# A streaming encoder step on one core: gain, mean and bias of the last normalization applied by TensorE, and other tiles in other buffers

## The chip, the cores and the metric

The kernel runs on one core of a Trainium2 chip. A run is one launch, and the time is the device time of that core in microseconds (us). Of the kernel before there are three runs, with a median of 2784.76 us, and one more execution that was profiled.

The engines are named as in the profile: PE is TensorE (PEld its weight loads), DVE is VectorE, ACT is ScalarE, POOL is GpSimd, SP the engine that issues most loads and stores. DMA stands for the transfers themselves. PSUM is the memory that products are written to, in eight banks of 512 columns; everything else on the chip lies in SBUF.

## The reference

One step of a two-layer encoder over 288 frames: 256 of a new stream and 32 of a running one. Each frame has 2048 features. The first layer mixes by a gated MLP, the second by retention; behind each comes a dense SwiGLU network (FFN), and behind each of these four parts a normalization:

```python
def layer_norm(x, g, b):
    mu = jnp.mean(x, axis=-1, keepdims=True)
    var = jnp.mean(jnp.square(x - mu), axis=-1, keepdims=True)
    return (x - mu) * lax.rsqrt(var + LN_EPS) * g + b

def swiglu(x, w_in, w_out):
    gate, up = jnp.split(x @ w_in, 2, axis=-1)
    return (jax.nn.silu(gate) * up) @ w_out

for i in range(2):
    h = gmlp_mix(x) if i == 0 else retention_mix(x)
    x = layer_norm(ALPHA * x + h, ln_mix_g[i], ln_mix_b[i])
    x = layer_norm(ALPHA * x + swiglu(x, w_ffn_in[i], w_ffn_out[i]), ln_ffn_g[i], ln_ffn_b[i])
```

The hidden width of the FFN is 5632. All is in 32-bit floats. The change concerns the last `layer_norm` alone, whose result is the output `y`.

## The kernel before

**Layout.** Activations are held with the features on the 128 partitions: 16 tiles (KT) of 128 features, each 128 x 288 with the frames as columns. A normalization over the features is therefore a sum over partitions and tiles; partitions are summed by a product with a constant matrix `one2048` that holds 1/2048, which leaves the mean of each frame in every partition.

**Weights.** All weight matrices are cut into blocks of 128x128 and packed in the order of use, eight blocks to a chunk of 512 KB. `prep` (L71) loads a chunk from DRAM into a tile `raw` on SP's queue, ScalarE casts it to a rounded high part `whi` (L559, in the helper `split`), VectorE subtracts to get the low part `wlo` (L560). The pool has three `raw` buffers, four `whi` and four `wlo`. `blk` (L90) asks for chunk c+3 when the first block of chunk c is taken.

**Products.** `step` (L110 to L112) makes three products of 288 columns per block: high by high, low activation by high weight, high activation by low weight. PE runs its instructions in the order in which they are written. The other engines' order is set by a planner that walks the program with estimated durations and lets an instruction go when what it needs is there, earlier written ones first. In a `manual_schedule` block the named engines too keep the written order.

**The two FFNs.** `ffn` (L704) makes half of the hidden tiles (22 of 44), multiplies them by their part of the output weights, then does the other half. In the second FFN a tile `hid` holds the high and low parts of the hidden tiles side by side. The last four output tiles (12 to 15, ENDS) of the second half are not made there but in `ending`.

**The ending.** `ending` (L424) first calls `ahead` (L331), then goes over tiles 12 to 15 and 22 hidden tiles each: a product of 288 columns with the low weight (L436) and a `paired` one (L437) that takes high and low hidden parts for the first half of the frames (144 columns of each). The weight chunks are kept: for the first seven, `whi` lies in room of the activation tiles `xl` and `xh`, which nobody needs any more. A second pass (`second`, L445) makes the `paired` products for the other half of the frames, 4 tiles x 22. So the first half of the frames (h = 0) is complete one pass earlier and is normalized while PE does the second pass.

From there on VectorE, ScalarE and POOL run in written order (FINISH). For each tile `add` brings the PSUM sums into `yh`, `square` squares on ScalarE, `gather` (L355) adds tile and square into two running sums on VectorE. `means` (L372) multiplies the sums by `one2048`; `spread` (L387 to L396) makes the row of means and the row `a` = 1/sqrt(variance + eps). `rows` (L401) subtracts the mean or multiplies by `a`, up to four tiles at a time, `affine` (L408 on ScalarE, L410 on VectorE) applies gain and bias per feature, `store` (L413) writes out.

For the second half (h = 1), behind the last tile, PE does the subtraction for nine tiles: `lift` (L420, L421) multiplies each by the identity and adds the negative mean by a matrix whose first row is -1. VectorE then multiplies from PSUM (L490) three tiles at a time. Identity and the -1 matrix lie in a tile `centring`, which `ahead` takes from the pool tag `raw`.

Of the kernel before, what the change touches and what calls it, by code (L numbers as in the profile page):

```python
# [210 lines left out]
class PostNorm:  # L211
# [118 lines left out]

    def ahead(self, ms):  # L331
        nc = self.nc
        for m in ms:
            nc.vector.tensor_tensor(self.tile(m), self.tile(m), self.like(self.c), ALU.subtract)
# [13 lines left out]
    def square(self, h, m):  # L348
        self.sq = self.tmp(f"sq{h}_{m}")[:, :NH]
        self.nc.scalar.activation(self.sq, self.yh[:, h, m, :], AF.Square)  # L350

    def gather(self, h, m):
        s = self.s[:, :, h * NH:(h + 1) * NH]
        for i, d in enumerate((self.yh[:, h, m, :], self.sq)):
            self.nc.vector.tensor_tensor(s[:, i, :], s[:, i, :], d, ALU.add)  # L355

    def end(self, h, m, ps):
        self.add(h, m, ps)
        self.square(h, m)
        self.gather(h, m)  # L360

    def first(self, m, ps, both):
        y = self.tile(m)
        self.nc.vector.tensor_tensor(y, self.like(both[:, :NT]), y, ALU.add)
        self.end(0, m, ps)

    def means(self, h, parts):
        core, one = self.core, self.cst["one2048"]
        self.m = [core.bank(f"m{h}{i}")[:, :NH] for i in range(2)]
        for j, p in enumerate(parts):  # L370
            for m, r in zip(self.m, p):
                self.nc.tensor.matmul(m, one, r, start=j == 0, stop=j == len(parts) - 1)  # L372
# [5 lines left out]
    def spread(self, h, mids, between):  # L378

        nc, core = self.nc, self.core  # L380
        cols = slice(h * NH, (h + 1) * NH)
        m1, m2 = self.m
        self.scale, self.mean = self.a[:, cols], self.b[:, cols]
        self.ap = ap = core.bank(f"ap{h}")[:, :NH]
        v = core.bank(f"fin{h}")[:, :NH]
        t, r = self.tmp(f"t{h}")[:, :NH], self.tmp(f"r{h}")[:, :NH]
        nc.scalar.activation(t, m1, AF.Square)  # L387
        nc.scalar.copy(self.mean, m1)
# [9 lines left out]
    def rows(self, h, k, n, eng, op):  # L398
        f = {ALU.subtract: (self.m[0], self.mean), ALU.mult: (self.ap, self.scale)}[op][eng is self.nc.gpsimd]
# [14 lines left out]

    def lift(self, h, k, n):

        mm = self.nc.tensor.matmul
        off = self.core.accum(f"off{k}")[:, :n * NH].rearrange("p (k n) -> p k n", n=NH)
        for i in range(n):
            mm(off[:, i, :], self.ident, self.yh[:, h, k + i, :], start=True, stop=False)  # L420
            mm(off[:, i, :], self.minus, self.mean, start=False, stop=True)  # L421
        return off

    def ending(self, w, koff, x):  # L424
# [24 lines left out]
        def quad(k, eng=dve):  # L449
            self.rows(0, k, 4, eng, ALU.subtract)  # L450
            self.rows(0, k, 4, eng, ALU.mult)

        def out(k):
            self.affine(0, k, 4)
            self.store(0, k, 4)

        with core.tc.manual_schedule(engines=FINISH):
# [17 lines left out]
            self.add(1, KT - 1, ps[KT - 1])  # L475
            self.square(1, KT - 1)
            self.means(1, [self.sum_rows(1), (self.yh[:, 1, KT - 1, :], self.sq)])
            off = {}

            def mids():  # L480
                for k in (2, 5, 8):
                    off[k] = self.lift(1, k, 3)
                self.rows(1, 12, 4, gps, ALU.subtract)

            self.spread(1, mids, lambda: self.rows(1, 0, 2, dve, ALU.subtract))
            self.rows(1, 12, 4, gps, ALU.mult)

            def lifted(k):
                y = self.yh[:, 1, k:k + 3, :]
                dve.tensor_tensor(y, off[k], self.scale.unsqueeze(1).broadcast_to([P, 3, NH]), ALU.mult)  # L490

            lifted(2)
            self.rows(1, 0, 2, dve, ALU.mult)
            self.affine(1, 2, 3)
            self.store(1, 2, 3)
            lifted(5)
            self.affine(1, 0, 2)
            self.store(1, 0, 2)
# [686 lines left out]
```

## Time and profile before

| | |
|---|---|
| median of the three runs | 2784.76 us (2783.88 to 2784.85) |
| the profiled execution, its own time | 2786.61 us |
| its span, first to last instruction | 2784.8 us |
| mean granted clock of TensorE | 0.998 |
| PE busy | 2771.0 us, 21,614 instructions |
| VectorE, ScalarE, POOL busy | 1702.9, 1252.3, 138.9 us |
| read and written in DRAM | 487 and 25 MB, 184 GB/s over the span |
| ending: first product, last large product | 2727.6 and 2765.6 us from the span's start |
| last store issued | 2781.2 us |

A row of the chain of waits is: start, duration, engine, what it writes, the line, and how many were merged. A row of the timeline is: start, duration, engine, line, operation, out<-in, shapes, count, and in brackets how long the engine had been idle before and what ended that. A row for a stretch has the stretch, its length, then the busy time of PE, PEld, DVE, ACT and POOL with their counts, the granted clock of TensorE (1.00 is full), the busy share of the DMA engines and GB/s. Products in 32-bit floats show as two records each; the large ones as one.

### The profile page before, as it was taken

What the parts mean: (1) busy time and instruction counts of PE and PEld (TensorE: products, weight loads), DVE (VectorE), ACT (ScalarE), POOL (GpSimd) and SP (SyncE); (2) the same over time, 40 slices, a digit from 0 to 9 for tenths busy, and PEclk for the clock granted to TensorE, in tenths of its full rate; (3) what the DMA queues carried; (4) which work ended last, traced back from release to release, by engine and by line L of the source; (5) the groups of instructions that cost most, each with busy time, mean ns of one, the idle gap of its engine ahead of it and who ended that gap; (6) DMA issues with size and microseconds to landing.
All of it is one profiled execution on the core that took longest, in us unless ns stands there. A gap on an engine that the chain in (4) does not pass through costs nothing.

```text
span 2784.8 us, 51601 instructions
## 1 busy us (share of the span) xinstructions
PE 2771.0 (100%) x21614; PEld 2760.1 (99%) x21614; DVE 1702.9 (61%) x2497; ACT 1252.3 (45%) x1680; POOL 138.9 (5%) x239
## 2 busy tenths in 40 slices
PE   9999999999999999999999999999999999999998
PEld 9999999999999999999999999999999999999997
DVE  6688964445444466968765676767954444444465
ACT  5455554333333344645443444445644333343344
POOL 1100000000000000012200111200000000000000
PEclk9999999999999999999999999999999999999999
DMA  8654555555555555567765676765555555555553
GB/s 279 219 186 163 171 174 175 174 174 174 172 174 172 179 177 175 176 216 233 225 208 172 197 224 205 233 199 173 168 174 174 174 168 173 174 172 173 173 174 110
DMA packets 146585, 515.51 MB, mean 185 GB/s; under 512 B 18016, under 2 KB 20464, under 8 KB 146320
## 3 DMA queue, kind: packets, MB, share of 16 engines
q1 hardware_dynamic: 131984, 473.33, 51.3%
q0 software_dynamic: 14224, 38.59, 4.7%
q8 instruction: 169, 2.77, 0.4%
q14 instruction: 64, 0.52, 0.1%
q10 hardware_dynamic: 144, 0.29, 0.0%
HBM read 486.98 MB, written 25.17 MB: 184 GB/s over the span
## 4 chain that ended last, share of the span: by engine, by line
PE 98%; DVE 1%; DMA 1%; ACT 0%; issue 0%; DVEq 0%; POOL 0%; ACTq 0%; POOLq 0%
PE af_in L110 13%; PE af_in L112 13%; PE af_in L111 13%; PE ab_in L110 7%; PE ab_in L112 7%; PE ab_in L111 7%; PE af_out L111 6%; PE af_out L112 6%; PE af_out L110 6%; PE aa_in L112 2%; PE aa_in L110 2%; PE aa_in L111 2%; PE ab_out L110 2%; PE ab_out L111 2%; PE ab_out L112 2%; PE aa_out L111 1%
## 5 line engine op out<-in xcount | busy, mean ns | idle before, releaser
L560 DVE TENSOR_TENSOR wlo<-raw,whi 128x1024 fp32r<-128x1024 f32 (+1 forms) x885 | 1076.1, 1218 | 851.1 <-ACT whi L559 846.4
L559 ACT CAST whi<-raw 128x1024 fp32r<-128x1024 f32 (+1 forms) x885 | 925.7, 1048 | 1320.8 <-PE af_in L111 324.2
L110 PE MATMUL af_in<-xh,whi 128*128 128x288 f32 (+1 forms) x2816 | 814.1, 289 | 0.0
L112 PE MATMUL af_in<-xh,wlo 128*128 128x288 f32 (+1 forms) x2816 | 813.8, 289 | 0.0
L111 PE MATMUL af_in<-xl,whi 128*128 128x288 f32 x2816 | 812.8, 289 | 0.0
L111 PEld LDWEIGHTS af_in<-xl,whi 128*128 128x128 f32 x2816 | 528.6, 188 | 0.0
L112 PEld LDWEIGHTS af_in<-xh,wlo 128*128 128x128 f32 x2816 | 528.6, 188 | 0.0
L110 PEld LDWEIGHTS af_in<-xh,whi 128*128 128x128 f32 x2816 | 528.4, 188 | 0.0
L110 PE MATMUL ab_in<-xh,whi 128*128 128x288 f32 (+1 forms) x1536 | 445.4, 290 | 0.0
L112 PE MATMUL ab_in<-xh,wlo 128*128 128x288 f32 (+1 forms) x1536 | 444.0, 289 | 0.0
L111 PE MATMUL ab_in<-xl,whi 128*128 128x288 f32 x1536 | 444.0, 289 | 0.0
L111 PEld LDWEIGHTS ab_in<-xl,whi 128*128 128x128 f32 x1536 | 288.4, 188 | 0.9
L110 PEld LDWEIGHTS ab_in<-xh,whi 128*128 128x128 f32 x1536 | 288.2, 188 | 0.8
L112 PEld LDWEIGHTS ab_in<-xh,wlo 128*128 128x128 f32 x1536 | 288.4, 188 | 0.0
L112 PE MATMUL af_out<-hh,wlo 128*128 128x288 f32 x704 | 203.2, 289 | 0.0
L110 PE MATMUL af_out<-hh,whi 128*128 128x288 f32 x704 | 203.2, 289 | 0.0
L111 PE MATMUL af_out<-hl,whi 128*128 128x288 f32 x704 | 203.2, 289 | 0.0
L111 PE MATMUL af_out<-hid,whi 128*128 128x288 f32 x616 | 179.6, 292 | 0.0
L112 PE MATMUL af_out<-hid,wlo 128*128 128x288 f32 x616 | 179.3, 291 | 0.0
L110 PE MATMUL af_out<-hid,whi 128*128 128x288 f32 x616 | 177.2, 288 | 0.0
L110 PE MATMUL aa_in<-xh,whi 128*128 128x288 f32 x512 | 148.4, 290 | 0.0
L112 PE MATMUL ab_out<-r_oh,wlo 128*128 128x288 f32 x512 | 147.8, 289 | 0.0
(281 smaller groups left out, 3806.1 us busy)
## 6 DMA issues: line engine op xcount, KB each, us to landing
raw<-in_wpack_dram SPq DMA_DIRECT2D x887, 512.0 KB, 3.3
v_room<-tv POOLq DMA_DIRECT2D x32, 144.0 KB, 4.9
of<-o_room POOLq DMA_DIRECT2D x32, 144.0 KB, 5.2
vw<-v_room POOLq DMA_DIRECT2D x8, 512.0 KB, 5.9
out_st_s_dram<-sso POOLq DMA_DIRECT2D x16, 256.0 KB, 2.7
o_room<-to POOLq DMA_DIRECT2D x8, 512.0 KB, 3.3
out_st_p_dram<-so POOLq DMA_DIRECT2D x16, 256.0 KB, 5.3
y<-in_xT_dram SPq DMA_DIRECT2D x8, 288.0 KB, 4.9
```

Source lines behind the costliest of these rows:

```text
L110: mm(wide, hi, halves(xh, lead), start=first, stop=False)
L111: mm(halves(ps[:, lead:], 0, lead), hi, halves(xl), start=False, stop=False)
L112: mm(wide, lo, halves(xh, lead), start=False, stop=last)
L559: nc.scalar.copy(hi, f)
L560: nc.vector.tensor_tensor(lo, f, hi.bitcast(F32), ALU.subtract)
```

## The change

- **Tables.** A new method `tables`, called when the second FFN opens its pool, makes there the identity, 15 diagonal 128x128 blocks of the gain (`diag`, 15 ScalarE scalings of the identity), a tile `gb` with the gain in row 0 and the bias in row 32 (zeroed on POOL, then two loads of 8 KB on POOL's queue from a new input), and a zeroed tile `ms` of 64 x 144. `hid` lies behind these in the same pool, and the filler tile ahead of it shrinks from 44 to 36 floats.
- **No `centring`.** `ahead` no longer takes a `raw` buffer; the -1 matrix is gone.
- **First half.** The means are asked for after product 15 of the second pass's first tile rather than 19. POOL subtracts and multiplies for tiles 8 to 15 (before: 12 to 15), VectorE for 0 to 7 (before: 0 to 11). `affine` of tiles 8 to 11 goes to VectorE.
- **Sums of the second half.** `gather` is gone there. Tiles 12 to 15 and their squares are summed by PE, each as a further product with `one2048`, together with the running sums of tiles 0 to 11.
- **The close.** For tiles 1 to 15 PE multiplies by the diagonal gain block (`gained`) and then adds gain x (-mean) + bias x standard deviation by one product with `gb` and `ms`. VectorE multiplies the result by `a` from PSUM, three tiles at a time, and it is stored. Tile 0 goes by VectorE and ScalarE. All stores are on SP.

```diff
+    def tables(self, pool, rows):
+        nc = self.nc
+        ident = pool.tile([P, P], F32, name="ident")
+        make_identity(nc, ident)
+        self.diag = pool.tile([P, KT, P], F32, name="diag")
+        for k in range(1, KT):
+            nc.scalar.mul(self.diag[:, k, :], ident, self.gain(k))
+        self.gb = pool.tile([2 * NS, KT, P], F32, name="gb")
+        self.ms = pool.tile([2 * NS, NH], F32, name="ms")
+        nc.gpsimd.memset(self.gb, 0.0)
+        nc.gpsimd.memset(self.ms, 0.0)
+        for i in range(2):
+            nc.gpsimd.dma_start(self.gb[i * NS:i * NS + 1], rows[i:i + 1])
+
     def ahead(self, ms):
...
-        room = self.core.wp.tile([P, CB * P], F32, tag="raw", name="centring", bufs=3)
-        self.ident, self.minus = room[:, :P], room[:, P:2 * P]
-        make_identity(nc, self.ident)
-        nc.gpsimd.memset(self.minus, 0.0)
-        nc.gpsimd.memset(self.minus[:1, :], -1.0)
...
+    def mean(self, i, r, start=False, stop=False):
+        self.nc.tensor.matmul(self.m[i], self.cst["one2048"], r, start=start, stop=stop)
...
         with core.tc.manual_schedule(engines=FINISH):
             self.first(KT - 1, *ps[KT - 1])
-            second(KT - 4, {19: lambda: self.means(0, [self.sum_rows(0)])})
-            self.spread(0, lambda: None, lambda: self.rows(0, 0, 4, dve, ALU.subtract))
-            quad(12, gps)
-            self.end(1, KT - 4, ps[KT - 4])
+            second(12, {15: early})
+            self.spread(mids, lambda: self.rows(0, 0, 4, dve, ALU.subtract))
+            for k in (8, 12):
+                self.rows(0, k, 4, gps, ALU.mult)
+            self.add(1, 12, ps[12])
+            sums = [self.sum_rows(1), self.square(1, 12)]
             self.rows(0, 0, 4, dve, ALU.mult)
             out(0)
-            second(KT - 3)
-            quad(4)
+            second(13)
+            for op in (ALU.subtract, ALU.mult):
+                self.rows(0, 4, 4, dve, op)
             out(4)
-            self.end(1, KT - 3, ps[KT - 3])
-            second(KT - 2)
-            quad(8)
-            out(8)
+            self.add(1, 13, ps[13])
+            sums.append(self.square(1, 13))
+            second(14)
+            self.add(1, 14, ps[14])
+            sums.append(self.square(1, 14))
+            out(8, dve)
             out(12)
-            self.end(1, KT - 2, ps[KT - 2])
-            second(KT - 1)
...
+            second(15)
+            self.close(ps[15], sums)
+
+    def close(self, b, sums):
+        core, nc, m = self.core, self.nc, KT - 1
+        mm, dve = nc.tensor.matmul, nc.vector
+        self.add(1, m, b)
+        y, sq = self.square(1, m)
+        self.means(1)
+        for j, pair in enumerate(sums):
+            for i, r in enumerate(pair):
+                self.mean(i, r, j == 0)
+        self.mean(0, y, stop=True)
+        off = {}
+
+        def gained(k):
+            bank = core.bank if k == 10 else core.accum
+            off[k] = bank(f"off{k}")[:, :3 * NH].rearrange("p (k n) -> p k n", n=NH)
+            for i in range(3):
+                mm(off[k][:, i, :], self.diag[:, k + i, :], self.yh[:, 1, k + i, :], start=i == 0, stop=False, skip_group_check=True)
...
+        self.mean(1, sq, stop=True)
+        for k in (4, 1, 7, 10, 13):
+            gained(k)
+        m1, m2 = self.m
+        std = slice(NS, NS + 1)
+        nc.scalar.activation(t, m1, AF.Square)
+        nc.scalar.mul(self.ms[:1], m1[:1], -1.0)
+        dve.tensor_tensor(self.yh[:, 1, 0, :], self.yh[:, 1, 0, :], m1, ALU.subtract)
+        dve.scalar_tensor_tensor(v, m2, LN_EPS, t, ALU.add, ALU.subtract)
+        nc.scalar.activation(r, v, AF.Abs_reciprocal_sqrt)
+        dve.tensor_tensor(p, v, r, ALU.mult)
+        dve.scalar_tensor_tensor(q, p, -0.5, r, ALU.mult, ALU.mult)
+        dve.scalar_tensor_tensor(self.ms[std], q[std], 1.5, p[std], ALU.add, ALU.mult)
+        dve.scalar_tensor_tensor(a, q, 1.5, r, ALU.add, ALU.mult)
+        for k in (4, 1, 7, 10, 13):
+            for i in range(3):
+                mm(off[k][:, i, :], self.gb[:, k + i, :], self.ms, start=False, stop=i == 2, skip_group_check=True)
+            y = self.yh[:, 1, k:k + 3, :]
+            dve.tensor_tensor(y, off[k], a.unsqueeze(1).broadcast_to([P, 3, NH]), ALU.mult)
+            if k == 4:
+                d = self.yh[:, 1, 0, :]
+                dve.tensor_tensor(d, d, a, ALU.mult)
+                self.affine(1, 0, 1)
+            first = 0 if k == 1 else k
+            self.store(1, first, k + 3 - first)
...
-            pool.tile([P, 44], F32, name="shift_hid")
+            ln.tables(pool, rows)
+            pool.tile([P, 36], F32, name="shift_hid")
             hid = pool.tile([P, HH, 2 * ROW], F32R, name="hid")[:, :, LEAD:]
```

More of the change, by code (lines that the diff above doesn't have):

```diff
@@ L348, in square @@
     def square(self, h, m):
[L349 to L360, printed above, removed]
+        sq = self.tmp(f"sq{h}_{m}")[:, :NH]
+        self.nc.scalar.activation(sq, self.yh[:, h, m, :], AF.Square)
+        return self.yh[:, h, m, :], sq
     def first(self, m, ps, both):
@@ L364, in first @@
         self.nc.vector.tensor_tensor(y, self.like(both[:, :NT]), y, ALU.add)
[L365 to L372, printed above, removed]
+        self.add(0, m, ps)
+        for s, d in zip(self.sum_rows(0), self.square(0, m)):
+            self.nc.vector.tensor_tensor(s, s, d, ALU.add)
     def sum_rows(self, h):
@@ L398, in rows @@
     def rows(self, h, k, n, eng, op):
-        f = {ALU.subtract: (self.m[0], self.mean), ALU.mult: (self.ap, self.scale)}[op][eng is self.nc.gpsimd]
+        f = {ALU.subtract: (self.m[0], self.mean_row), ALU.mult: (self.ap, self.scale)}[op][eng is self.nc.gpsimd]
         y = self.yh[:, h, k:k + n, :]
@@ L447, in second, with early, out, mids @@
                     at[k]()
[L449 to L454, printed above, removed]
+        def early():
+            self.means(0)
+            for i, s in enumerate(self.sum_rows(0)):
+                self.mean(i, s, True, True)
+        def out(k, eng=None):
+            self.affine(0, k, 4, eng)
             self.store(0, k, 4)
+        def mids():
+            for k in (8, 12):
+                self.rows(0, k, 4, gps, ALU.subtract)
@@ L474, in ending @@
-            second(KT - 1)
[L475 to L498, printed above, removed]
-            lifted(8)
-            self.rows(1, 11, 1, dve, ALU.subtract)
-            self.rows(1, 11, 1, dve, ALU.mult)
@@ L701, in gmlp, with ffn @@
     return ln
-def ffn(core, cst, x, y, lnp, layer, prev, out=None):
+def ffn(core, cst, x, y, lnp, layer, prev, out=None, rows=None):
     tc, nc = core.tc, core.nc
```

41 lines of the change are left out of this document (16 added, 25 removed).

## The prediction

> **What bounds the kernel now.** I read the page first, then the chain of waits, the load queue, the stretches of the granted clock, and last the timeline of the end.
>
> ```profile
> span 2784.8 us, 51601 instructions
> PE 98%; DVE 1%; DMA 1%; ACT 0%; issue 0%; DVEq 0%; POOL 0%; ACTq 0%; POOLq 0%
> ```
>
> The span is one stream of TensorE products. What can be won without touching their number lies where the chain leaves PE, and that is in the last 45 us:
>
> ```profile
> 2743.24 4.63 DMA raw<-in_wpack_dram
> 2747.97 1.05 ACT whi L559
> 2749.05 1.24 DVE wlo L560
> 2750.33 0.40 PE q L436
> ...
> 2767.33 3.29 ACT y L408 x8
> 2770.62 0.22 ACT sq L350
> 2770.87 0.32 DVE sums L355
> 2771.23 1.89 PE m L372 x6
> ...
> 2778.63 0.61 DVE y L490
> ```
>
> Two places. First, the last weight chunk comes late: its load (4.63 us), cast and split, and PE waits. Second, after its last large product PE waits for eight ScalarE `affine`s (3.29 us), behind which the square and sum of tile 14 are queued.
>
> Why the load is late is in the timeline of the weight loads, VectorE's splits and the casts, with a load 50 us earlier, the queue's own waits (us in total, times, longest) and the page's row for the load (us to landing):
>
> ```profile
> 2690.65 0.33 SPq L78 DMA_DIRECT2D raw<-in_wpack_dram  x1
> 2697.30 1.05 ACT L559 CAST whi<-raw 128x1024 fp32r<-128x1024 f32 x1 [1.52 <-PE af_out L111]
> 2741.99 1.23 DVE L560 TENSOR_TENSOR wlo<-raw,whi 128x1024 fp32r<-128x1024 f32 x1 [0.95 <-ACT whi L559]
> 2743.24 0.33 SPq L78 DMA_DIRECT2D raw<-in_wpack_dram  x1
> SPq L78 <- DVE wlo L560: 27.8, 10, 3.8
> raw<-in_wpack_dram SPq DMA_DIRECT2D x887, 512.0 KB, 3.3
> ```
>
> The last load is issued at 2743.24, just when the split of the chunk two before it ends (2741.99 + 1.23). At 2690.65 a load was issued 6.65 us ahead of its cast, and that cast waited for PE, not for data. The pool of `raw` tiles has three buffers (L81); `ahead` (L334) takes one of them for `centring` and keeps it to the end, because `lift` reads it. From there two loads are in flight. Here SP is bound by buffers.
>
> The stretches (PE busy, PEld, DVE, ACT, POOL; then the clock):
>
> ```profile
> 2747.80:2751.10 3.30, 1.49 (x12) 1.27 (x11) 1.66 (x3) 1.27 (x2) 0.00 (x0) 1.00 0.00 0
> 2751.20:2754.50 3.30, 3.30 (x16) 3.30 (x15) 0.77 (x2) 0.00 (x0) 0.00 (x0) 0.50 0.00 0
> 2768.30:2771.60 3.30, 1.18 (x3) 0.83 (x4) 0.70 (x3) 2.54 (x7) 0.00 (x0) 0.50 0.26 96
> ```
>
> Each wait is paid twice: a stretch in which PE was busy 1.49 of 3.30 us is followed by one at clock 0.50, and the wait before the means puts them at half clock too.
>
> **The change part by part.**
>
> *The third `raw` buffer.* `ahead` no longer takes `centring`; its identity goes into the FFN's own pool. Loads may again be issued three chunks ahead. The waiting time (the split's end, then 4.7 us to the cast, then 2.3 us of cast and split) spread over three buffers is 2.3 us a chunk, 1.9 us for the usual load of 3.3; PE uses a chunk in 2.02 (16 products of 126.5 ns, below). With the lead of some 7 us that is worked out under the tables, 0.3 us a chunk at worst does not use it up in eight chunks. So PE runs through:
>
> ```profile
> 2365.00:2620.00 255.00, 255.00 (x2015) 1.00 0.52 174
> 2727.58 0.29 PE L436 MATMUL q<-hid,wlo 128*128 128x288 f32 x1
> 2765.10 0.80 PE L445 MATMUL b<-hid,whi 128*128 128x288 f32 x5
> 2775.24 0.41 PE L421 MATMUL off<-b,centring 128*128 128x144 f32 x2
> 2778.18 0.41 PE L421 MATMUL off<-b,centring 128*128 128x144 f32 x2
> ```
>
> A product of 288 columns takes 255 / 2015 = 126.5 ns. The ending's 4 x 22 x 2 + 4 x 22 = 264 products take 33.4 us, the two sum products of the first half 0.49 more: from 2727.58 PE is done at 2761.5. Before, the last of the five products in the third row began at 2765.61, so PE was done at 2765.74. Gain 4.2 us: 1.8 of wait (1.49 busy of 3.30), 1.7 of half clock, small pieces.
>
> By the Trainium skill, "TensorE: Matmul & The Clock Gate", section "What's actually happening", the clock halves only after a whole idle window of about 3.4 us. The trace differs: half clock after a wait of 1.8 us. If the rule held, only the waits would come back, 1.7 less, and the time would be about 2777.4.
>
> *The first half's normalization moves.* POOL now takes tiles 8 to 15 (four operations for two), VectorE does `affine` for 8 to 11, ScalarE for the other twelve, and the two gathers per tile (L355) go.
>
> ```profile
> 2757.13 0.29 ACT L387 ACTIVATE t<-m 128x144 f32<-128x144 f32 x1 [1.95 <-PE m L372]
> 2757.68 1.43 POOL L401 TENSOR_TENSOR y<-y,b 128x576 f32<-128x576 f32 x1 [36.07 <-ACT b L388]
> 2759.04 0.31 DVE L395 SCALAR_TENSOR_TENSOR a<-ap,r 128x144 f32<-128x144 f32 x1
> ```
>
> Count from the start of the second pass, which ends 11.6 us later (4 x 2.79 + 0.49). The means come at 2.6 (they are asked for 4 products earlier), the scale at 4.9 (the 2.2 us of the rows at 2757.13 and 2759.04). POOL starts at 3.2 and needs 4 x 1.43: done at 8.95. ScalarE, 0.41 an `affine` (3.29 / 8), does tiles 0 to 7 by 9.7, squares 13 and 14 by 10.3, tiles 12 to 15 by 11.9. VectorE does 8 to 11 by 11.0, then waits for PE. So nothing is queued ahead of tile 15: its two adds and its square, 0.31 each like the row at 2759.04, run from 11.8 to 12.9. Cost nothing; the cover is 0.7 us on ScalarE, and if POOL runs 2 us longer, as much goes onto the end.
>
> *The close.* The sums of tiles 12 to 14 go to PE unsummed: with `sum_rows` four pairs, then tile 15: 10 fp32 products, where there were 4. Then 15 tiles by the diagonal of the gain (`gained`) and 15 by `gb` and `ms`: 30 where there were 18. One takes 0.245 us at full clock ((2778.18 - 2775.24) / 12). PE has no wait before them: eight sum products last to 13.6, the square of tile 15 is there at 12.9. So full clock stays, and the 40 take 9.8 us: PE is done at 2771.3. The row `ms` they need goes ScalarE, VectorE five operations of 0.31 and a square root: ready at about 16.5, while `gained` lasts to 17.8. Hidden, with 1.3 us to spare. VectorE multiplies three tiles in 0.61 (L490) each 0.735 us of PE, so PE leads. Last multiply: 0.2 us after PE, 0.61 long: 2772.1. `affine`, subtract and second multiply are gone but for tile 0.
>
> *The last store.* One of 216 KB on SP, where 288 KB on ScalarE's queue came last:
>
> ```profile
> 2780.32 0.79 DVE y L410 x3
> 2781.18 0.37 ACTq L413 DMA_DIRECT2D out_yT_dram<-y  x1
> 2782.10:2783.05 0.95, 0.00 (x0) 0.00 (x0) 0.00 (x0) 0.00 (x0) 0.00 (x0) 0.50 0.97 371
> 2783.05:2784.80 1.75, 0.00 (x0) 0.00 (x0) 0.00 (x0) 0.00 (x0) 0.00 (x0) 0.50 0.00 0
> ```
>
> Issue 0.07 after VectorE, data 0.92 later, 216 KB at 371 GB/s 0.6, then 1.75 to the span's end: 3.35 us. Stores every 0.74 us don't pile up. End at 2775.4 for 2784.8: 9.4 us less.
>
> *The tables.* `ln.tables` at the start of the second FFN: identity, two memsets and two small loads on POOL, which has nothing else there, and 15 ScalarE scalings of 128x128.
>
> ```profile
> 1950.00:1955.00 5.00, 5.00 (x42) 5.00 (x41) 3.46 (x8) 2.27 (x3) 0.00 (x0) 1.00 0.51 152
> 1955.00:1960.00 5.00, 5.00 (x41) 5.00 (x41) 4.22 (x7) 2.47 (x6) 0.38 (x1) 1.00 0.47 163
> 1959.85 0.68 PE L321 MATMUL m<-s,one_r 128*128 128x288 f32 x4
> 1959.11 0.45 DVE L560 TENSOR_TENSOR s<-sums,s 128x288 fp32r<-128x288 f32 x1
> ```
>
> At 0.29 to 0.41 each (ScalarE's square at 2757.13, its `affine`) they take 4 to 6 us; ScalarE has 5.3 idle in these ten. Its casts wait for PE (the row at 2697.30): with four `whi` buffers a chunk is cast some three chunks ahead, 3 x 3.04 us (24 products each), and split 2.3 later, a lead of some 7 us. But the statistics of the norm before have only 0.29 us between their last split (1959.56) and PE. Four scalings of 0.41 in front of it would cost 1.4 us, none nothing; I take 0.3, as a scaling already running holds each of ScalarE's two casts there by part of one.
>
> *The hidden tile moves* by 512 + 8192 + 8192 + 576 + 144 - 176 = 17,440 bytes. All 1,848 products of the last projection ahead of the ending read it.
>
> ```profile
> 2235.00:2355.00 120.00, 120.00 (x933) 1.00 0.51 172
> 2635.00:2725.00 90.00, 90.00 (x708) 1.00 0.50 165
> ```
>
> They run at 128.6 and 127.1 ns where the input projection runs at 126.5, so something of this tile costs 2.7 us (1056 x 2.1 + 792 x 0.6 ns). At best that goes. At worst the rows show no bound; one more step of 2.1 ns above 128.6 for all of them would cost 5.1 (1056 x 2.1 + 792 x 3.6). I take 0, the rate that the same tile has now.
>
> By the Trainium skill, "SBUF — State Buffer", section "Specifications (TRN2)", what counts is 16-byte lines, and 17,440 is a multiple of 16: the move would be free, 2775.7. The trace has one address with two rates, so it neither shows nor excludes that.
>
> **Sum.** 2784.8 - 4.2 (loads and clock) - 5.2 (close and store) + 0.3 = 2775.7 of span. The profiled execution took 2786.61, 1.85 above the median 2784.76; the same 9.1 us off the median gives 2775.7.
>
> **The rivals.**
> - *The loads stay late* (the last one's 4.63 us against 3.3 says that they can be slow by themselves). PE is done at 2765.74 as now, the rest holds: 2780.0, within 0.2%. Against it: the SP rows wait for splits, not for the DMA.
> - *The moved tile is slower*, by up to the 5.1 us above: 2780.8, also within 0.2%.
> - *The other side: the moved tile is much slower.* From 4.9 ns a product (9.1 / 1848) the gain is gone, from 8 ns (14.7 / 1848), that is 136 ns, the kernel is slower by over 0.2%: 10 ns give 2794. For it: this is the one tile whose products already differ from the rest. Against: the spread shown is 2.1 ns.
> - *The tables hold ScalarE* until the last tile of the retention's output projection lets their memory go, with casts queued behind: what exceeds the lead of about 7 us stalls PE. A hold of 16 us uses up the gain, 22 us makes it slower (2790.4). Against: what these tables wait for is released by PE itself, within the last product of that projection that reads it.
>
> **How the numbers follow.** Forecast 0.76, late loads 0.08, tile slower 0.06, tile much slower 0.06, tables 0.04 (half within, half slower). 0.2% is 5.6 us, about what a measurement of this kernel can tell from none: faster 0.76, same 0.16, slower 0.08. Range: down to 2772.3 (the tile at full rate, the tables free, 0.5 for spread), up to 2780.8 (the two rivals within).
>
> **What would show it.** No PE wait on `wlo` after 2740 and no stretch at clock 0.50 before the last product; loads issued at least 5 us ahead of their cast; `gained` right behind the sums, at 0.245 a product; the last multiply about 10.6 us after the last large product; no new PE wait near 1955. The forecast is wrong if products on `hid` leave 127 to 129 ns, if POOL ends after PE's second pass, or if the casts still wait for data.

## The result, and the profile after

The kernel after takes 2775.24 us (median of 7 runs, 2774.62 to 2777.95). The kernel before, run beside it on the same chip, takes 2785.17 us (7 runs, 2783.88 to 2787.66). The ratio is 0.9965, with a 95% interval of 0.9953 to 0.9977: 6.4 to 13.1 us less. The forecast was 2775.7. The profiled execution of the kernel after took 2774.66 us, its span is 2772.6 where that of before was 2784.8.

From the page of the kernel after: span, busy times, and the share of the span in the chain that ended last.

```profile
span 2772.6 us, 51660 instructions
PE 2767.6 (100%) x21650; PEld 2757.4 (99%) x21650; DVE 1700.4 (61%) x2489; ACT 1250.3 (45%) x1680; POOL 142.0 (5%) x241
PE 100%; DMA 0%; DVE 0%; ACT 0%; SPq 0%; issue 0%
```

The chain stays on PE: VectorE and DMA, 1% each before, are below half a per cent. The end of the chain (start, us, engine, what it writes, line):

```profile
2749.57 9.12 PE b L435 x72
2758.68 2.45 PE m L376 x20
2761.14 3.67 PE off L493 x30
2764.81 3.88 PE off L515 x30
2768.72 0.61 DVE y L517
```

No wait stands between the second pass (`b`), the sums (`m`) and the 60 records of `off`. The first 20 records of sums after the pass are 10 products: 0.245 us each, the price that the forecast used. The stretches of the same time (length; busy PE, PEld, DVE, ACT, POOL; clock, DMA share, GB/s):

```profile
2755.00:2760.00 5.00, 5.00 (x43) 5.00 (x42) 2.29 (x8) 3.64 (x10) 0.55 (x1) 1.00 0.52 194
2760.00:2765.00 5.00, 5.00 (x42) 4.86 (x41) 1.76 (x6) 0.74 (x3) 0.00 (x0) 1.00 0.12 46
```

PE is busy throughout, and the granted clock stays at 1.00 up to 2772.4, behind its last product, where the kernel before had stretches at 0.50 both behind its wait for the last chunk and before its means.

To see where the 12.2 us between the two spans went, the span was cut at the first product of each stage. The second pass is taken to end 0.127 us after its last product starts, when the next one could start at full rate. Every stage between the first input projection and the last output projection agrees within 0.04 us. What differs, in us:

| stage | before | after | difference | forecast |
|---|---|---|---|---|
| opening and first input projection | 208.10 | 207.26 | -0.84 | none |
| input projection of the second FFN, first half (tables) | 269.10 | 269.12 | 0.0 | +0.3 |
| its output, first half: 16 tiles x 22 blocks | 136.11 | 133.76 | -2.35 | 0 |
| its output, second half: 12 tiles x 22 blocks | 101.19 | 101.33 | +0.14 | 0 |
| ending, first pass | 26.04 | 22.30 | -3.74 | both passes |
| ending, second pass | 12.12 | 11.65 | -0.47 | -4.2 |
| close: from the end of the second pass to the span's end | 19.02 | 14.03 | -4.99 | -5.2 |

The opening is no effect of the change. It varies from run to run: its first input projection alone took 202.2 to 205.5 us over the profiled executions of all kernels of this study, on no pattern that follows the edits. So single spans are compared below stage by stage.

### The profile page after: what moved, and what is told of

Same layout as the page of the kernel before. It is cut to its first block, busy times and chain, and to the rows that moved or that the text cites. A ratio compares the mean times of both kernels' runs of the same rounds, so it can differ in the third digit from the quotient of the medians.

```text
span 2772.6 us, 51660 instructions
## 1 busy us (share of the span) xinstructions
PE 2767.6 (100%) x21650; PEld 2757.4 (99%) x21650; DVE 1700.4 (61%) x2489; ACT 1250.3 (45%) x1680; POOL 142.0 (5%) x241
## 4 chain that ended last, share of the span: by engine, by line
PE 100%; DMA 0%; DVE 0%; ACT 0%; SPq 0%; issue 0%
PE af_in L112 13%; PE af_in L110 13%; PE af_in L111 13%; PE ab_in L110 7%; PE ab_in L112 7%; PE ab_in L111 7%; PE af_out L112 6%; PE af_out L110 6%; PE af_out L111 6%; PE aa_in L111 2%; PE aa_in L112 2%; PE ab_out L112 2%; PE ab_out L111 2%; PE ab_out L110 2%; PE aa_in L110 2%; PE aa_out L110 1%
## 5 line engine op out<-in xcount | busy, mean ns | idle before, releaser
L111 PE MATMUL aa_in<-xl,whi 128*128 128x288 f32 x512 | 147.7, 289 | 0.1
```

Of the source, the lines that this page charges most:

```text
L111: mm(halves(ps[:, lead:], 0, lead), hi, halves(xl), start=False, stop=False)
```

## The experiments

In each, "ending" is the time from its first product to the span's end (57.18 before, 47.97 after). The ratios are against the kernel before, run beside them.

**The buffer, taken away again.** This is the kernel after with one `raw` buffer held through the ending.

```diff
     def ahead(self, ms):
...
+        self.held = self.core.wp.tile([P, CB * P], F32, tag="raw", name="held", bufs=3)
+        self.nc.gpsimd.memset(self.held[:, :P], 0.0)
...
     def close(self, b, sums):
...
+        nc.gpsimd.memset(self.held[:, :P], 0.0)
```

> The changed kernel, with one of the three raw buffers taken at the start of the ending and kept to the close, as centring was. If the third buffer is what let PE run through: PE waits again for the last low weight part (some 2 us), the next stretch runs at clock 0.50 (1.7 us), and the time is about 4.2 us more than the changed kernel's, 0.15%. If the last load of the kernel before was slow by itself, or the whole gain lies in the close: within 0.5 us of the changed kernel, with no PE wait.

2780.25 us, ratio 0.9973 (0.9963 to 0.9984). The wait for the split is back, in PE's waits (us in total, times, longest):

```profile
PE q L428 <- DVE wlo L577: 0.7, 2, 0.4
```

But it is 0.7 us only, the first pass 23.58 (after 22.30), the ending 49.25: 1.3 longer, not 4.2. The same kernel was run once more to see how firm that is.

> hold_raw once more, unchanged. Up to the ending its program is the changed kernel's instruction for instruction, with the hidden tile at the same address, and yet its last projection ran at 383.3 ns for three products where the changed kernel had 380.0. If the rate goes with the loaded program: 134.9 and 101.0 us for the two parts again. If PE falls into one of the rates by chance: 133.8 or 136.1 can come.

```profile
PE q L428 <- DVE wlo L577: 1.8, 2, 1.5
```

Now the wait is 1.8 us, the first pass 24.63 and the ending 50.31: 2.3 longer. What the held buffer costs depends on how long the last load happens to take: from issue to cast 3.52 us in the first of these two, 4.47 in the second, 4.73 in the kernel before; the three loads ahead of it take 3.2 to 3.5. In neither execution did the clock fall behind the wait. So neither expectation came: the wait is there, at a third to a half of the 4.2. The median of the seven runs, 2780.25, lies 2.8 above the profiled one of 2777.49, so these stages are those of a short run; by the ratios the two kernels can't be told apart.

**The buffer, freed in the kernel before.** The identity goes into the FFN's pool, and nothing else of the change is made.

```diff
-        room = self.core.wp.tile([P, CB * P], F32, tag="raw", name="centring", bufs=3)
+        room = self.pool.tile([P, 2 * P], F32, name="centring")
...
             if ends:
+                ln.pool = pool
                 ln.ending(f"f_out{layer}", half * HH, hid)
```

> The kernel before, with centring in the FFN's own pool behind all its other tiles, so that the three raw buffers stay free; the hidden tile does not move. If the buffer is the cause: no PE wait on the last low part, full clock to the end of the second pass, 4.2 us less than the kernel before (2781). If not: the same as the kernel before.

2783.14 us, ratio 0.9987 (0.9979 to 0.9996). No wait for a split is left, and the two passes take 22.30 and 11.66, 4.2 us less, to the digit what the forecast gave. Yet the ending is 3.1 shorter only (54.09), because the close became 1.1 longer (20.13). Its end in the chain:

```profile
2766.28 3.29 ACT y L408 x8
...
2770.18 1.89 PE m L372 x6
2772.07 0.48 PE off L420 x2
...
2776.43 0.25 PE off L421 x2
```

ScalarE's eight `affine`s still hold up the sums, and the last sums begin 5.6 us after the start of the last large product, as before. PE waits twice for them:

```profile
PE m L372 <- DVE sums L355: 4.8, 2, 2.5
```

What is new is that the `lift` products (L420, L421) stay at 0.48 us for a pair of records until 2776.4, 4.4 us after the first of them. In the chain of the kernel before they were at 0.24 from 2775.40 on, 2.3 us after the first. The stretches at half clock, first of the kernel before, then of this one (PE busy and its products come first):

```profile
2768.24:2775.07 6.83, 4.69 (x17) 4.22 (x18) 2.44 (x8) 3.74 (x12) 1.42 (x2) 0.50 0.24 89
2769.43:2776.26 6.83, 6.08 (x24) 5.96 (x25) 3.42 (x10) 2.26 (x9) 2.80 (x2) 0.50 0.15 55
```

The half clock is as long in both, but it ends 9.5 us after the last large product starts in the kernel before and 11.7 us after it here. So it covers less of PE's waits and 2.2 us more of its products, and half of that is the 1.1 us. The loads' gain is thus a term of its own, and what reaches the span's end depends on where the half clock lies in the close.

**The address, moved in the kernel before.** A longer filler puts `hid` at the address that it has in the kernel after, 17,440 bytes up; nothing else differs from before.

```diff
-            pool.tile([P, 44], F32, name="shift_hid")
+            pool.tile([P, 4408], F32, name="shift_hid")
```

> The kernel before, with a filler of 4408 floats ahead of the hidden tile, which puts it at the very address that it has in the changed kernel; nothing else. If the address decides the rate of the products on it: the first 16 output tiles take 133.8 us for 136.1, the other 12 take 101.3 for 101.2, and the time is 2.2 us less. If a multiple of 16 bytes changes nothing, and the faster products of the changed kernel come from elsewhere: 136.1 and 101.2, time the same.

2784.99 us, ratio 0.9992 (0.9983 to 1.0001). The two parts of the last output projection take 133.76 and 101.33, the very values of the kernel after. A stretch of 120 us in the first of them (products as PE's count):

```profile
2239.00:2359.00 120.00, 120.00 (x950) 120.00 (x949) 61.71 (x70) 41.16 (x40) 0.00 (x0) 1.00 0.54 176
```

950 products where the kernel before had 933. So moving `hid` alone gives the -2.35 and the +0.14. (One address can show two states 0.8 us apart, as the last section has it.) That the time stayed is no contradiction: the expected gain of 2.2 us lies within the interval.

The same kernel says something on the clock. It has the wait for the last chunk as before (1.84 us of idle PE, 1.81 in the kernel before), and right behind it:

```profile
2751.60:2755.00 3.40, 3.40 (x27) 3.40 (x27) 1.44 (x5) 0.00 (x0) 0.00 (x0) 1.00 0.00 0
```

Full clock, 27 products in 3.4 us where the kernel before had 16. Its passes take 25.20 and 11.65.

**The address, 32 bytes down and 32 bytes up in the kernel after.**

```diff
-            pool.tile([P, 36], F32, name="shift_hid")
+            pool.tile([P, 28], F32, name="shift_hid")
```

> The changed kernel with 28 floats of filler for 36: the hidden tile lies 32 bytes lower, at the remainder (32 of 128 bytes) that it had in the kernel before. If the remainder by 128 decides: the first 16 output tiles take 136.1 us again and the time is 2.2 us more than the changed kernel's. If the place as a whole or nothing of it decides: 133.8 us as in the changed kernel, time the same.

2777.48 us, ratio 0.9968 (0.9957 to 0.998). The parts take 134.94 and 101.33: between the two expectations, 1.2 us more than after. The first part has this value in some executions at the address of the kernel after too (last section), so one profiled execution doesn't show that the 32 bytes made it.

```diff
-            pool.tile([P, 36], F32, name="shift_hid")
+            pool.tile([P, 44], F32, name="shift_hid")
```

> The changed kernel with 44 floats of filler for 36, as the kernel before has: the hidden tile 32 bytes higher. If the address alone decides the rate of the last projection: a value of its own for the first 16 output tiles, the same at each run; the three seen are 133.8, 134.9 and 136.1 us. If it does not matter: 133.8.

2782.51 us in one execution, 137.28 and 102.58: 4.8 us more than after, and values that no other execution has. The second pass of the ending, which reads the same tile, takes 12.12 for 11.65, at full clock. The stretches of 120 us, first of the kernel after, then of the one 32 bytes down, then of the one 32 bytes up:

```profile
2234.20:2354.20 120.00, 120.00 (x949) 120.00 (x948) 60.86 (x70) 42.00 (x40) 0.00 (x0) 1.00 0.52 174
```

```profile
2236.00:2356.00 120.00, 120.00 (x941) 120.00 (x941) 60.48 (x69) 41.43 (x40) 0.00 (x0) 1.00 0.53 172
```

```profile
2239.00:2359.00 120.00, 120.00 (x925) 120.00 (x924) 59.74 (x69) 40.14 (x39) 0.00 (x0) 1.00 0.49 168
```

949, 941 and 925 products in the same time, with the DMA, the engines and the clock alike.

**Full clock through the means, in the kernel before.** PE is given 18 products whose result nobody uses, while it waits for the running sums and again between the two sums.

```diff
...
+            fill = core.accum("fill")
+
+            def keep_busy():
+                for k in range(18):
+                    mm(halves(fill), hi[KT - 1, k], paired(x, k, 1), start=k == 0, stop=k == 17)
+
+            keep_busy()
...
-            self.means(1, [self.sum_rows(1), (self.yh[:, 1, KT - 1, :], self.sq)])
+            self.means(1, [self.sum_rows(1), (self.yh[:, 1, KT - 1, :], self.sq)], keep_busy)
```

> The kernel before, with 18 extra products (2.3 us) in each of PE's two waits ahead of the means; their result is not used. If it is the idling that halves the clock: no stretch at 0.50 in the close, sum and off products at 0.245 for 0.48, and the last multiply from PSUM comes 1.5 to 1.9 us earlier, counted from the end of the second pass. If the clock halves for another reason: the stretches at 0.50 stay, and nothing is won.

2784.04 us, ratio 0.9991 (0.9982 to 1.0001). The stretches, the first behind the wait for the last chunk, the others around the means:

```profile
2749.90:2753.30 3.40, 3.40 (x26) 3.40 (x27) 1.44 (x5) 0.00 (x0) 0.00 (x0) 1.00 0.00 0
2767.10:2770.50 3.40, 3.16 (x23) 2.66 (x22) 0.83 (x3) 2.16 (x7) 0.00 (x0) 1.00 0.46 174
2770.50:2773.90 3.40, 3.30 (x28) 3.11 (x27) 2.58 (x7) 1.64 (x6) 2.75 (x2) 1.00 0.00 0
```

The clock holds at 1.00 through the close, and the last multiply ends 12.34 us after the end of the second pass, 1.2 sooner than in the two kernels with `centring` in a `raw` buffer and no fillers (13.5 and 13.6). That is less than the 1.5 to 1.9 expected. The fillers did not hold PE up: the last of them starts at 2768.71, and the second running sum comes at 2769.14, as late behind the second pass as in the kernel before. But with the clock full the chain then runs over VectorE's two adds of tile 15 (0.55 us) before the next sums. So of the 2.7 us by which the change brought the last multiply forward (13.5 to 10.80), a little under half is the clock. The other 1.5 is left for the wait on the `affine`s and VectorE's adds, which no run took apart. The first row is a second case of full clock behind a wait for the last chunk, of 1.88 us by the timeline.

**The sums on VectorE again.** In the kernel after, VectorE adds tiles 12 to 14 and their squares to the running sums again, as before the change, and PE makes six sum products fewer.

```diff
...
             self.add(1, 12, ps[12])
-            sums = [self.sum_rows(1), self.square(1, 12)]
+            self.gather(12, self.square(1, 12))
+            sums = [self.sum_rows(1)]
...
-            sums.append(self.square(1, 13))
+            self.gather(13, self.square(1, 13))
...
-            sums.append(self.square(1, 14))
+            self.gather(14, self.square(1, 14))
```

> The changed kernel with the running sums of tiles 12 to 14 of the second half added up on VectorE again (gather, two operations a tile with both inputs in SBUF, written behind each square), so that PE has 4 sum products in the close for 10. If VectorE and POOL shut each other out there (the row of 1.14 us for a sum of 0.31 in the kernel before, which ended with POOL's operation): tile 12's gather stands in POOL's four operations, VectorE loses 0.6 to 2.4 us, ScalarE's affines start that much later, and the end comes 0.5 to 2 us later than in the changed kernel. If not: PE's close is six products shorter and waits only for the square of tile 15: 0.7 us earlier.

2779.24 us, ratio 0.9974 (0.9964 to 0.9984): six products fewer, and the ending 3.0 us longer (50.94), more than expected. Timeline rows, of POOL, VectorE and PE (start, duration, engine, line, operation; idle time before in brackets):

```profile
2750.57 2.82 POOL L404 TENSOR_TENSOR y<-y,b 128x576 f32<-128x576 f32 x2 [790.59 <-ACT b L391]
2753.36 2.95 POOL L404 TENSOR_TENSOR y<-y,a 128x576 f32<-128x576 f32 x2
2752.83 0.73 DVE L363 TENSOR_TENSOR sums<-sums,y 128x144 f32<-128x144 f32 x1
2753.48 1.53 DVE L363 TENSOR_TENSOR sums<-sums,sq 128x144 f32<-128x144 f32 x1
2757.72 0.31 DVE L363 TENSOR_TENSOR sums<-sums,y 128x144 f32<-128x144 f32 x1
2760.52 0.93 PE L380 MATMUL m<-sums,one 128*128 128x144 f32 x4 [1.23 <-DVE sums L363]
2762.56 0.84 PE L380 MATMUL m<-y,one 128*128 128x144 f32 x2 [1.11 <-DVE y L354]
2763.68 4.72 PE L498 MATMUL off<-y,diag 128*128 128x144 f32 x30
```

Beside POOL's subtractions and multiplies a sum of two SBUF operands takes VectorE 0.73 and 1.53 us; once POOL is done, the same sum takes 0.31. That is 1.6 us lost. VectorE then also idles 1.23 us for tile 13's square, which ScalarE makes behind its `affine`s, and tile 15's adds come behind all that: PE waits twice, 1.23 and 1.11 us. Then half clock: the gain blocks take 4.72 us, 3.84 in the same view of the kernel after. What the sums would cost without POOL beside them, no run shows. Six products of 0.245 would have been 1.5 us less. The Trainium skill, "SBUF — State Buffer", section "SBUF: two separate sides", has a VectorE instruction with two SBUF inputs and a GpSimd instruction that reads SBUF exclude each other for the whole of an instruction. The 0.73 and 1.53 for 0.31 agree.

**ScalarE's cover.** The `affine`s of tiles 8 to 11 stay on ScalarE, where the change gives them to VectorE.

```diff
-            out(8, dve)
+            out(8)
```

> The changed kernel with the affines of tiles 8 to 11 of the first half on ScalarE instead of VectorE, four more of 0.41 us ahead of tile 15's square. In the changed kernel PE reaches that square's product 1.0 us after the square is done. If PE's products bound the close and ScalarE is only cover: the square comes 0 to 0.7 us too late for PE, and the end by as much. If ScalarE's work counted in full: 1.65 us later.

2775.75 us in one execution, the ending 47.97: nothing changes, the lower end of the first expectation. From the timeline:

```profile
2758.17 3.28 ACT L407 ACTIVATE y<-y,lnv 128x144 f32<-128x144 f32 x8
2761.36 0.31 ACT L358 ACTIVATE sq<-y 128x144 f32<-128x144 f32 x1
2761.99 0.41 PE L376 MATMUL m<-sq,one 128*128 128x144 f32 x2
```

Even behind eight `affine`s the square of tile 15 (done at 2761.67) is 0.3 us ahead of PE, which the 10 sum products keep busy until then. So this part of the change bought a margin and no time.

**A shorter close.** Tiles 12 to 15 are normalized by POOL (subtract, multiply) and ScalarE (`affine`), so PE makes 24 products there instead of 30.

```diff
-        for k in range(1, KT):
+        for k in range(KT - 4):
             nc.scalar.mul(self.diag[:, k, :], ident, self.gain(k))
...
-        for k in (4, 1, 7, 10, 13):
+        ks = (0, 3, 6, 9)
+        for k in ks:
             gained(k)
...
+        nc.scalar.copy(self.mean_row, m1)
+        self.ap = None
+        self.rows(1, 12, 4, nc.gpsimd, ALU.subtract)
...
+        self.rows(1, 12, 4, nc.gpsimd, ALU.mult)
...
+            if k == 6:
+                self.affine(1, 12, 4)
+            self.store(1, k, 3)
+            if k == 6:
+                self.store(1, 12, 4, nc.scalar)
```

> The changed kernel with tiles 12 to 15 of the second half subtracted and multiplied by POOL and scaled by ScalarE in the close, both of which idle there, and PE taking 0 to 11: 24 products for 30, no tile left to VectorE. If the close is bound by PE's products alone: the last multiply from PSUM 1.5 us earlier after the last large product (9.1 for 10.6), and the time 0.05% under the changed kernel's, too little for the runs to tell. If the row ms or POOL's tiles come last: 0 to 1 us less won, or lost.

2775.73 us, ratio 0.9963 (0.995 to 0.9975). The last multiply ends 9.33 us after the end of the second pass, 1.47 sooner, as six products of 0.245 give. The last multiply comes as the first expectation had it (1.5), but the ending is 0.8 shorter only (47.14): the rest goes to stores that now come closer together than they run. One more thing is in its timeline, POOL's subtract and the operation of VectorE beside it:

```profile
2764.14 1.41 POOL L400 TENSOR_TENSOR y<-y,b 128x576 f32<-128x576 f32 x1 [6.12 <-ACT b L508]
2764.79 0.93 DVE L514 SCALAR_TENSOR_TENSOR fin<-p,r 128x144 f32<-128x144 f32 x1
```

0.93 us for an operation of 0.31, again with two SBUF operands beside POOL. The second version puts one operand (`p`) in PSUM and stores tiles 12 to 15 earlier.

```diff
...
-        v, q = fin[:, :NH], fin[:, NH:NT]
-        t, r, p = (self.tmp(n)[:, :NH] for n in ("t1", "r1", "p1"))
+        v = fin[:, :NH]
+        t, r, q = (self.tmp(n)[:, :NH] for n in ("t1", "r1", "q1"))
+        p = fin[:, NH:NT]
```

> better, with the products of the variance's root arranged so that each VectorE operation but one reads one input from PSUM while POOL subtracts, and the store of tiles 12 to 15 issued ahead of the last three-tile stores. If POOL's operation held VectorE's second one there (0.93 us for 0.31): it takes 0.31, the row ms is ready before PE is through with the gain blocks, and the end comes 1.2 to 1.5 us earlier than in the changed kernel, counted from the first product of the ending (better: 0.8). If the stores at the end are what is left: the same as better.

```profile
2764.25 0.31 DVE L515 SCALAR_TENSOR_TENSOR q<-fin,r 128x144 f32<-128x144 f32 x1
```

The operation is back at 0.31, but PE's last product does not come sooner, so it was hidden, and the second expectation came: about the same as the version before. 2774.63 us, ratio 0.9961 (0.9947 to 0.9975), the ending 47.05, 0.9 less than after; from the last multiply to the span's end it is 3.77 us, 3.22 in the kernel after, and the 0.55 is stores. By its stages this is the shortest of the endings; by its times it cannot be told from the kernel after. That one was also profiled once more, to see how far its stages repeat.

> The changed kernel once more. If the hidden tile's address fixes the rate of the last projection: 133.8 us for the first 16 output tiles and 101.3 for the other 12, as at the first look. If the rate is one of several that PE falls into (386.7, 383.3, 380.0 ns for three products have been seen, 383.3 at the same address with hold_raw): another of them, 133.8, 134.9 or 136.1.

2775.44 us, 133.77 and 101.32, ending 47.97: all within 0.01 us of the first execution.

## Why the prediction was right, and where its terms were off

- **The third buffer, -4.2.** Right to the digit: -3.74 and -0.47 in the two passes, and the same when the buffer alone was freed in the kernel before. The mechanism was the one given. The leads of the chunks (from the end of the split to PE's use) fell from 7.1 to 0.06 us over the last ten or so chunks before; after, they fall from 7.8 to 3.2 and end at 3.5. So the lead was not used up, as said, but the loss was mis-sized: 0.65 us a chunk over the first seven, where the prediction had 0.3 at worst; over the last four it holds at 3.2 to 3.7. The composition of the 4.2 was partly luck: about 0.9 in the first pass and 0.5 in the second (26.04 and 12.12 against 25.1 to 25.2 and 11.65 with the buffer held and the clock full) was half clock that two other kernels with the like wait did not have. Against an execution of the kernel before without it, the gain would be some 2.8 (4.2 less 1.4), which is worked out and not measured.
- **The sign "loads issued at least 5 us ahead of their cast".** Wrong: 3.4 to 4.8 for the last four chunks. SP still waits for splits, and casts of the last chunks for data (waits of SP's queue from 2700 us on; a load; the cast of its chunk):

```profile
SPq L78 <- DVE wlo L574: 29.3, 12, 3.1
```

```profile
2735.64 0.33 SPq L78 DMA_DIRECT2D raw<-in_wpack_dram  x1
2739.00 1.06 ACT L573 CAST whi<-raw 128x1024 fp32r<-128x1024 f32 x1 [0.41 <-DMA raw<-in_wpack_dram]
```

  The cover is the lead carried in from the projection, not the loads' own distance. The prediction had named casts that wait for data as a sign that it is wrong, and products on `hid` outside 127 to 129 ns as another. Both came (126.7 ns in the first part, 380.0 / 3), and yet the forecast held: PE did not see the first, and the second went the good way. So these two were badly chosen signs.
- **The close and store, -5.2.** Measured -4.99. 40 products in 9.9 us (forecast 9.8), the last multiply ending 10.80 us after the end of the second pass (10.6), then 3.22 us to the end (3.35). Of the gain, 2.7 us lie ahead of that multiply's end and 2.3 behind it: in the kernel before VectorE worked on for 1.9 us (to 2781.11, the prediction's row at 2780.32), and the rest is the smaller store.
- **The covers named.** ScalarE's square of tile 15 ends at 2759.73, PE takes it at 2760.73: 1.0 us where 0.7 was said. The row `ms` is there at 2763.41, PE needs it at 2764.74: 1.3, as said. POOL ends at 2755.55, 8.7 us after the second pass begins (8.95):

```profile
2752.73 2.82 POOL L400 TENSOR_TENSOR y<-y,a 128x576 f32<-128x576 f32 x2
2759.41 0.32 ACT L358 ACTIVATE sq<-y 128x144 f32<-128x144 f32 x1 [0.81 <-DVE y L354]
2760.73 0.41 PE L376 MATMUL m<-sq,one 128*128 128x144 f32 x2
2763.11 0.30 DVE L511 SCALAR_TENSOR_TENSOR ms<-fin,p 1x144 f32<-1x144 f32 x1
2764.74 3.94 PE L515 MATMUL off<-ms,gb 64*128 64x144 f32 x30
```

- **The tables, +0.3.** Measured 0.0 (269.12 for 269.10). The 15 scalings came behind the statistics that were feared for, in one block:

```profile
1960.10 0.41 ACT L326 ACTIVATE t<-m 128x288 f32<-128x288 f32 x1
1960.40 4.50 ACT L337 ACTIVATE diag<-ident,lnv 128x128 f32<-128x128 f32 x15
```

  They hold ScalarE for 4.5 us, and PE does not see it.
- **The moved tile, 0.** This is the term of the sum that was mis-sized: -2.2, or -1.4 in the other state of this address, inside its bounds of -2.7 and +5.1. That the place of this tile bears on the rate was the right suspicion: moving it alone in the kernel before gave both values, and the first part took 136.11 us in all three executions at the old address, 133.76 or 134.94 in all nine at the new one. The upper bound was not idle either: the same kernel 32 bytes higher pays 4.8 us against the kernel after, 2.6 against the kernel before.
- **The sum.** By stages the change is worth 9.2 in the ending and 2.2 at the tile, 11.4 us; the forecast had 9.1. The forecast time of 2775.7 stands nearer to the measured 2775.24 than its terms deserve, because the medians differ by 9.9 only, with an interval of 6.4 to 13.1 that holds both.
- **The rule on the clock.** The prediction set the Trainium skill's rule, "TensorE: Matmul & The Clock Gate", section "What's actually happening", against the trace: halved only after an idle window of about 3.4 us. The kernel before shows half clock behind a wait of 1.81 us, against the rule; three other executions show none behind waits of 1.5 to 1.9 us, so the row was no constant either. The same section has the window free-running, not started by the wait. The traces agree. The granted clock steps at multiples of 3.41 us, so each trace can be cut into windows by its steps. These are the windows with the most of the wait for the last chunk, of the kernel before, of the one with `hid` moved, of the one with fillers and of the second with the held buffer (PE busy comes first):

```profile
2747.77:2751.18 3.41, 1.60 (x12) 1.38 (x12) 1.66 (x3) 1.27 (x2) 0.00 (x0) 1.00 0.00 0
2747.66:2751.07 3.41, 2.10 (x16) 1.88 (x15) 1.06 (x2) 1.27 (x2) 0.00 (x0) 1.00 0.02 7
2748.59:2752.00 3.41, 2.11 (x16) 2.11 (x17) 1.66 (x3) 0.21 (x1) 0.00 (x0) 1.00 0.00 0
2744.68:2748.10 3.42, 2.06 (x16) 1.83 (x15) 1.36 (x2) 1.27 (x2) 0.00 (x0) 1.00 0.01 5
```

  In the kernel before the whole wait fell into one window, which left PE 1.60 us of work, and the next window ran at half clock. In the others an edge cut the wait in two, PE was busy for 2.06 us or more in the worse window, and the clock stayed. So behind these four waits the place of the wait in the windows decided, not its length. The limit between 1.60 and 2.06 is no general one: at the very end of the kernel 32 bytes up, a window with PE busy for 2.61 us was followed by half clock.

## What to carry to other kernels

When a trace shows the same instruction at two rates, the operand's address is a candidate that one filler can test, before any explanation by engines or transfers; put a price with a sign on moving such a tile. Where PE waits, count what the clock does behind the wait as a chance and not as a constant: here waits of nearly the same length did or did not halve it, by where they fell in windows of 3.41 us. Look for the work that can be queued on PE itself to close the gap: here six more sum products, 1.5 us of PE, took the place of two waits of 4.5 us in sum. A transfer queue may lose ground on every chunk and still be hidden: what counts is the lead at the start and the number of chunks.

## What the runs showed of the hardware that was not expected

**Products at fixed rates.** Three products of 288 columns that read `hid` (one block of weights) start 380.0, 383.3, 386.7 or 390.0 ns after the three before them, values 3.33 ns apart, and keep to one of these for whole tiles. In the kernel before it is 386.7, then 380.0 behind the fifth tile of the second part; after, 380.0 and then 383.3; 32 bytes down 383.3 throughout; 32 bytes up 390.0 and 386.7. The bytes at which `hid` starts are, modulo 128, 32 for the kernel before, 64 after, 32 and 96 for the two moved. So the residue does not decide alone: 32 stands for both 386.7 and 383.3. Nor does the address fix it: of nine executions with `hid` where the kernel after has it, five took 133.76 and 101.33, four 134.94 and 100.96, and the kernel with the held buffer, one program, did the one and the other. Its two stretches:

```profile
2235.00:2355.00 120.00, 120.00 (x942) 120.00 (x941) 60.54 (x69) 41.46 (x40) 0.00 (x0) 1.00 0.52 172
```

```profile
2235.00:2355.00 120.00, 120.00 (x949) 120.00 (x948) 60.50 (x69) 42.00 (x40) 0.00 (x0) 1.00 0.51 173
```

942 and 949 products in the same 120 us. The two states differ by 0.8 us in sum (235.9 and 235.1), less than the 2.2 of the change or the 4.8 of the 32 bytes. The Trainium skill, "SBUF — State Buffer", section "Specifications (TRN2)", has lines of 16 bytes; 32 bytes are a multiple of that, and the kernel 32 bytes higher still differs by 4.8 us, so that rule does not cover this. So the address bears on which rates come (12 executions at two addresses show no overlap in the first part), and something else picks among them. Why PE falls into these rates, and what picks the state, stays open.

**The last load.** It took 4.73 us to its cast in the kernel before and 4.77 with the tile moved, but 3.52 and 4.47 in the two executions of the kernel after with the buffer held. It is part of why the held buffer cost 1.3 and 2.3 us there instead of 4.2; the half clock of the kernel before is the other part. Why the last load takes so long is open.
